# A hybrid recurrent and attention block on one core: two attention row blocks under way, and blocks of the second and third pair asked for at other times

## The chip, the cores and the metric

The kernel runs on one core of one Trainium2 chip. The metric is the device time of one execution in microseconds (us). Engines are named as in the profile: PE (TensorE matmul), PEld (its weight loads), DVE (VectorE), ACT (ScalarE), POOL (GpSimd) and SP (SyncE, which issues most DMAs).

## The reference

One layer of a streaming encoder. 16 learned tokens are put ahead of 512 input tokens, so T = 528, with 1024 features each. All is float32.

```python
u = rmsnorm(h, norm_mix)
proj = u @ w_in                                  # 1024 x 5384
feat_rw, feat_fx, gates = ...                    # 1792, 1544 and 2048 columns
y_rw = rwkv7_branch(feat_rw)                     # 8 heads of 64: a recurrence over all tokens
y_fx = fox_branch(feat_fx)                       # 8 heads of 64: causal attention with forgetting
g = sigmoid(gates + b_gate)
merged = g[:1024] * (y_rw @ w_out_rw) + g[1024:] * (y_fx @ w_out_fx)
h = h + merged @ w_o
h = h + square(relu(rmsnorm(h, norm_mlp) @ w_up)) @ w_down
```

The attention of one head: query and key are normalised over their 64 features; the logit of row q and column k gets F[q] - F[k], a running sum of log sigmoids, and a causal mask; then softmax and the product with the values. The recurrent branch updates a 64 x 64 state a token at a time: `S = S * w + (S a) b + v k`, `y = S r`.

## The kernel before

Products of the large matrices are float32 as three passes: each operand is split into a high half (written by ACT) and a low half (written by DVE), and high x high, high x low and low x high are added up on PE. Tokens lie along the free dimension.

The part that the change touches is the stage from about 30 to 423 us of the span. It holds nearly all of the projections by `w_in`, the attention and the recurrence. Heads are worked on in pairs, 128 features wide, four pairs (0 to 3 in the code; first to fourth in the text) in either branch. The recurrence takes its pairs two at a time, in two groups, since each group is one chain of nine chunks of 64 tokens.

The stage is written as streams: Python generators that emit instructions and yield what they need next, an event or a time. `Turns.run` (L165) is a planner: it keeps a model of the clock (`Clock`, L63), always lets the stream of the lowest rank go on whose need is met, and so fixes the order of PE's instructions, which PE then follows. The streams and their ranks:

- rank 0, `chain` (L917): the nine chunks of a group of the recurrence, in which PE, DVE and ACT take turns
- rank 1, `recurrent` (L1021): for each pair its decay, keys, rows and scores, then `inverse` (L843) of the group's small triangular matrices, which is work for DVE above all
- rank 2, `attention` (L608): for each pair, one after the other, the four row blocks of 128 queries. `scored(i)` (L622) multiplies queries and keys (L631) and does the softmax on DVE and ACT (L640 to L647); `turned(i, pes)` (L651) transposes the weights on PE (L661, L663) and copies them out (L666 to L669); `mixed` (L671) multiplies them by the values (L676, L679)
- rank 3, `fox_features` (L545): for each pair the normalised query and key (L573) and the transposed values (L599, L602)
- rank 4, `divided` (L534) and `group_norm` (L985), the latter with L1003 and L1006
- rank 8, `projections` (L480): 24 blocks of 128 columns of `w_in` for the branches and 16 blocks for the gates. This is the bulk of the matmuls (L506), and what the planner puts on PE where no other stream can go on

A block is asked for with `ask` (L450), which puts it into a list by rank: blocks of the recurrence 1, of attention 2, gates 9. `projections` takes the first of the list, and works ahead: while one block's matmuls go on, the next is being converted (L475 on ACT, L476 on DVE) and the one after it loaded (L462). A block may have a `need`, an event; when its turn comes and the event isn't done, `projections` waits there, with everything behind it.

What is asked when, before: each attention pair asks for its query, key and values when `fox_features` comes to it, so those of the second pair when the first pair's are done; those of the third and fourth pair after `fox_near[p - 2]`, which is set when the last row block of the pair two before has been scored. Buffers set this: query and key tiles have two, and the squares and values share a ring of two (tag `fsq`). The third pair's recurrent values are asked for when the first inverse is through, with the need that the first chain has read the old ones (`values_read[0]`).

In `attention` a row block is scored, then transposed, then the next one is scored.

After the stage come the output projections (L1097), `w_o` (L1128, L1158), the first half of the MLP (L1186) and the second (L1313). There the sums of `w_down` blocks (L1235) read tiles `traw`, 16 of which are loaded by POOL's own DMA queue (L1223).

The functions that the diff touches:

Of the kernel before, what the change touches and what calls it, by code (L numbers as in the profile page):

```python
# [19 lines left out]
T = 528  # L20
# [167 lines left out]
def kernel(ctx, tc, ht, x, win, par, cst, gain, lora, wout, wo, wup, wdn, out, dbg=None):  # L188
# [97 lines left out]
    with ExitStack() as st:  # L286
# [147 lines left out]
        def banks(n):  # L434
            return ck.ring("sm", n, 4)
# [98 lines left out]
        def divided():  # L534
# [7 lines left out]
            for k in range(2, 4):  # L542
                split(*two(0, k), y_rw[:, k, :])

        def fox_features():  # L545
            for p in range(4):
                b0 = B_PAIR + 6 * p
                if p > 1:
                    yield fox_near[p - 2]

                def ask_normed(blk, parts, name, need=None):
                    d = {}

                    def begin():
                        c0 = parts[0][0]
                        d["f"] = f = fp.tile([128, T - c0], F32, name=name, bufs=2)
                        d["sq"] = sq = fp.tile([128, T], F32, name="fsq", tag="fsq", bufs=2)

                        def evac(po, sl):
                            d["s"] = act(sq[:, sl], po, AF.Square)  # L560
                            A.copy(f[:, sl.start - c0:sl.stop - c0], po)
                        return evac
                    d["in"] = ask(2, blk, begin, parts, need)
                    return d

                def normed(d, parts, gcol):
                    yield d["in"]
                    f, sq = d["f"], d["sq"]
                    yield lambda: max(ck.ready(sq), banks(len(parts)))
                    pin = None  # L570
                    for a0, a1 in parts:
                        pq = psm("pssq")[:, :a1 - a0]
                        mm(pq, ones_blk, sq[:, a0:a1], start=True, stop=True)  # L573
                        pin = pin or pinned(d["s"])
                        after(act(sq[:, a0:a1], pq, AF.Ln, bias=eps, scale=1.0 / 64), pin)
                    c0 = parts[0][0]
                    act(sq[:, c0:], sq[:, c0:], AF.Exp, scale=-0.5)
                    V.scalar_tensor_tensor(f, f, gcol, sq[:, c0:], ALU.mult, ALU.mult)
                    return f

                whole = ((0, HT), (HT, T))
# [3 lines left out]
                def begin():  # L585
                    d["v"] = fp.tile([128, T], F32, name="vf", tag="fsq", bufs=2)
                    return lambda po, sl: A.copy(d["v"][:, sl], po)
# [5 lines left out]
                vf = d["v"]  # L593
                yield lambda: max(ck.ready(vf), banks(2))
                vt = fp.tile([128, 4, 128], F32, name="vt", bufs=2)
                vm = fp.tile([48, 128], F32, name="vm", bufs=2)
                pv = psm("pv")
                for j in range(4):
                    nc.tensor.transpose(pv[:, 128 * j:128 * j + 128], vf[:, NM + 128 * j:NM + 128 * j + 128], ident)  # L599
                A.copy(vt.rearrange("p a b -> p (a b)"), pv)  # L600
                pvm = psm("pvm")
                nc.tensor.transpose(pvm[:16, :128], vf[:, :NM], ident)  # L602
                for e, hs in enumerate(hss):
                    A.copy(vm[32 * e:32 * e + 16, hs], pvm[:16, hs])
                fox_tiles[p] = q, k, vt, vm
                fox_ready[p].done = True

        def attention():  # L608
            for p in range(4):
# [12 lines left out]
                def scored(i):  # L622

                    n = NM + 128 * (i + 1)
                    parts = [(0, n)] if n <= 512 else [(0, n - 256), (n - 256, n)]
                    yield lambda: max(ck.ready(q, k), banks(2 * len(parts)))
                    scs = [[], []]
                    for a, b in parts:
                        for e, hs in enumerate(hss):
                            sc = psm("psc")[:, :b - a]  # L630
                            mm(sc, q[hs, 128 * i:128 * i + 128], k[hs, a:b], start=True, stop=True)  # L631
                            scs[e].append((sc, a, b))
                    pes = []
                    for e in range(2):
                        pe = fp.tile([128, T], F32, name="pe", bufs=2)
                        nm = fp.tile([128, 2], F32, name="nm", bufs=3)
                        least = 3e38
                        for x, (sc, a, b) in enumerate(scs[e]):
                            if b == n:
                                V.tensor_tensor(sc[:, b - a - 128:], sc[:, b - a - 128:], cmask, ALU.add)  # L640

                            V.tensor_tensor_reduce(pe[:, a:b], sc, along[e][:, a:b], -1.0, least, ALU.add, ALU.min, nm[:, x:x + 1])
# [4 lines left out]
                        V.tensor_scalar(pe[:, :n], pe[:, :n], rsum, None, ALU.mult)  # L647
                        pes.append(pe)
                    return pes
# [77 lines left out]
        class Pair:  # L727
            def __init__(self, p):
                self.p, self.b0 = p, B_PAIR + 6 * p + 3
# [187 lines left out]
        def chain(g, prs):  # L917
# [21 lines left out]
            for c in range(NCH):  # L939
# [76 lines left out]

        inverted = [Event() for g in range(2)]
        values_read = [Event() for g in range(2)]
        chained = [Event() for g in range(2)]
# [425 lines left out]
```

## Time and profile before

| | us |
|---|---|
| median of 3 runs | 847.93 |
| lowest and highest run | 847.22, 848.41 |
| the profiled execution | 848.62 |
| its span, from the first to the last instruction | 846.8 |
| PE busy | 829.4 (98%) |
| DVE busy | 626.7 (74%) |
| ACT busy | 458.1 (54%) |
| POOL busy | 117.7 (14%) |
| mean granted clock | 0.996 |

The profile is of one execution. A row of a group of instructions reads: line, engine, operation, tile written and tiles read, shapes, count, then busy us, mean ns of one, idle us of the engine just before them, and what ended it. A row of the timeline reads: start us, us, engine, line, operation, tiles, count, and in brackets how long the engine had been idle and what it waited for. PE's matmuls overlap: the time that one takes to the next is shorter than its duration. A row of a stretch gives its length, the busy time of PE, PEld, DVE, ACT and POOL (with counts), the granted clock of PE, the share of the DMA engines and GB/s.

### The profile page before, as it was taken

Reading aid. Unit: us, or ns where it says so; the run is one execution under the profiler, and the core shown is the slowest. Engines: PE = TensorE matmul, PEld = TensorE weight load, DVE = VectorE, ACT = ScalarE, POOL = GpSimd, SP = SyncE. Lnnn points to the kernel's source line nnn. Section 1 sums busy time; section 2 is a strip of 40 time slices with the busy share of each in tenths; the row PEclk is TensorE's granted clock in tenths of the full one; section 3 lists DMA queues with packets and bytes.
Section 4 is the critical chain, followed back from the end, with each engine's and each line's share of the span. In section 5 each row is a group of like instructions: output and inputs, shape, how many; then the busy total and the mean of one; then the engine's idle time right before and its main releaser. Section 6 shows DMA issues by size and latency. Waiting matters only on the chain.

```text
span 846.8 us, 15315 instructions
## 1 busy us (share of the span) xinstructions
PE 829.4 (98%) x5752; PEld 681.9 (81%) x5752; DVE 626.7 (74%) x1227; ACT 458.1 (54%) x946; POOL 117.7 (14%) x121
## 2 busy tenths in 40 slices
PE   7899999999999999999899999999999999999998
PEld 6888977878878867877588889888888888888886
DVE  6996986679899457666467544875898679867988
ACT  7767537765764356655366432665345444543452
POOL 1010200001010000000022101200560065007300
PEclk9999999999999999999899999999999999999999
DMA  6131231202112231143577402640753175327531
GB/s 229 56 106 54 76 101 42 77 27 64 53 61 74 90 101 52 38 137 101 175 253 248 145 26 87 187 125 26 253 170 100 51 248 152 97 93 217 155 108 74
DMA packets 51482, 95.88 MB, mean 113 GB/s; under 512 B 5832, under 2 KB 7240, under 8 KB 51408
## 3 DMA queue, kind: packets, MB, share of 16 engines
q1 hardware_dynamic: 47680, 86.38, 32.1%
q0 software_dynamic: 1280, 4.20, 1.7%
q10 hardware_dynamic: 2448, 4.33, 1.5%
q8 instruction: 45, 0.74, 0.4%
q14 instruction: 29, 0.24, 0.1%
HBM read 88.57 MB, written 6.31 MB: 112 GB/s over the span
## 4 chain that ended last, share of the span: by engine, by line
PE 84%; DVE 7%; ACT 3%; issue 2%; DMA 1%; DVEq 0%; ACTq 0%
PE po L1186 21%; PE pj L506 21%; PE po L1313 12%; PE po L1097 5%; PE pd L1313 5%; PE po L1158 3%; PE pw L884 2%; PE py L679 1%; PE psc L631 1%; PE pd L1128 1%; PE po L1128 1%; PE ppt L663 1%; PE psr L831 1%; DVE wlo L476 1%; PE pch L950 1%
## 5 line engine op out<-in xcount | busy, mean ns | idle before, releaser
L506 PE MATMUL pj<-uhi,whi 128*128 128x264 f32 (+1 forms) x480 | 165.7, 345 | 0.0
L506 PE MATMUL pj<-ulo,whi 128*128 128x264 f32 (+1 forms) x480 | 154.0, 321 | 1.5 <-DVE ulo L406 1.5
L506 PE MATMUL pj<-uhi,wlo 128*128 128x264 f32 (+1 forms) x480 | 153.9, 321 | 0.0
L239 DVE TENSOR_TENSOR wlo<-wraw,whi 128x512 fp32r<-128x512 f32 x88 | 91.9, 1054 | 28.8 <-ACT whi L238 28.7
L506 PEld LDWEIGHTS pj<-uhi,whi 128*128 128x128 f32 x480 | 90.2, 188 | 14.4 <-issue 5.5
L506 PEld LDWEIGHTS pj<-ulo,whi 128*128 128x128 f32 x480 | 90.4, 188 | 8.4 <-DVE ulo L406 1.9
L506 PEld LDWEIGHTS pj<-uhi,wlo 128*128 128x128 f32 x480 | 90.3, 188 | 6.9
L1186 PE MATMUL po<-zhi,whi 128*128 128x512 f32 (+1 forms) x248 | 94.8, 382 | 0.0
L1186 PE MATMUL po<-zlo,whi 128*128 128x512 f32 (+1 forms) x248 | 94.8, 382 | 0.0
L1186 PE MATMUL po<-zhi,wlo 128*128 128x512 f32 (+1 forms) x248 | 94.8, 382 | 0.0
L238 ACT CAST whi<-wraw 128x512 fp32r<-128x512 f32 x88 | 53.8, 617 | 55.9 <-PE po L1186 23.5
L476 DVE TENSOR_TENSOR wlo<-wraw,whi 128x512 fp32r<-128x512 f32 x80 | 55.5, 699 | 27.1 <-ACT whi L475 26.7
L475 ACT CAST whi<-wraw 128x512 fp32r<-128x512 f32 x80 | 49.0, 617 | 42.3 <-PE pj L506 41.6
L273 ACT CAST whi<-t 128x512 fp32r<-128x512 f32 x64 | 39.9, 624 | 44.5 <-DVE wlo L274 27.2
L1313 PE MATMUL po<-wlo,fhi 128*128 128x512 f32 (+1 forms) x164 | 63.4, 387 | 0.1
L1313 PE MATMUL po<-whi,flo 128*128 128x512 f32 (+1 forms) x164 | 62.8, 384 | 0.0
L1313 PE MATMUL po<-whi,fhi 128*128 128x512 f32 (+1 forms) x164 | 62.3, 384 | 0.0
L274 DVE TENSOR_TENSOR wlo<-t,whi 128x512 fp32r<-128x512 f32 x64 | 43.6, 690 | 24.3 <-ACT whi L273 24.0
L1235 POOL TENSOR_TENSOR t<-traw 128x512 f32<-128x512 f32 x24 | 36.4, 1525 | 176.1 <-DMA traw<-in_wdn 175.5
L1186 PEld LDWEIGHTS po<-zhi,whi 128*128 128x128 f32 x248 | 46.6, 188 | 9.0
L1186 PEld LDWEIGHTS po<-zhi,wlo 128*128 128x128 f32 x248 | 46.6, 188 | 9.0
L1186 PEld LDWEIGHTS po<-zlo,whi 128*128 128x128 f32 x248 | 46.6, 188 | 9.0
(307 smaller groups left out, 1740.2 us busy)
## 6 DMA issues: line engine op xcount, KB each, us to landing
wraw<-in_win SPq DMA_DIRECT2D x84, 256.0 KB, 2.6
wraw<-in_wup SPq DMA_DIRECT2D x60, 256.0 KB, 3.0
wraw<-in_wdn SPq DMA_DIRECT2D x48, 256.0 KB, 2.6
traw<-in_wdn SPq DMA_DIRECT2D x48, 256.0 KB, 3.3
gd<-gt ACTq DMA_DIRECT2D x16, 256.0 KB, 2.3
wraw<-in_wout SPq DMA_DIRECT2D x16, 256.0 KB, 3.4
gl<-gd SPq DMA_DIRECT2D x16, 256.0 KB, 3.4
traw<-in_wdn POOLq DMA_DIRECT2D x16, 256.0 KB, 3.1
```

The source lines that it names most:

```text
L238: A.copy(hi, raw)
L239: low.tensor_tensor(lo, raw, hi.bitcast(F32), ALU.subtract)
L273: A.copy(hi, x)
L274: V.tensor_tensor(lo, x, hi.bitcast(F32), ALU.subtract)
L475: A.copy(hi, raw)
L476: low.tensor_tensor(lo, raw, hi.bitcast(F32), ALU.subtract)
L506: mm(po, a, b[:, k, a0:a1], start=n == 0, stop=n == 23)
L1097: mm(po, a, ys[k][:, b, :], start=n == 0, stop=n == 11)
L1158: mm(po, a[:, k, 128 * i:128 * i + 128], b[:, k, :], start=n == 0, stop=n == 23)
L1186: mm(po[:, t0:t1], a, b[:, k, t0:t1], start=n == 0, stop=n == 23)
L1235: eng.tensor_tensor(t, sums[c, pair] if c in (T1, T2) else c, d, ALU.add)
L1313: mm(x[i][:, cols], a[:, k, left, 128 * rows:128 * rows + 128], c[:, cols], start=start and k == 0 and n == 0, stop=stop and k == n_pairs ...
```

## The change

Five edits:

1. `fox_features` is split into a class. The first pair's three blocks are asked for at the start as before, and with them the second pair's query (it needs the first pair's key to be done, `k_done`) and key (it needs the first pair's values, `v_done`). The second pair's values are asked for when the loop comes to it. The third and fourth pair ask as before.
2. `attention` scores the next row block before it transposes the present one. `fox_near` is set ahead of the third block's transposes, not behind them.
3. The softmax tile gets two names, for even and odd row blocks, two buffers each, the even one 128 columns shorter.
4. The third pair's recurrent values are asked for by the chain itself, at the point where `values_read[0]` is set, without a need. `recurrent` waits for that event before it uses them.
5. The scratch for DMAs that POOL issues is 4096 instead of 8192.

```diff
         def fox_features():
-            for p in range(4):
-                b0 = B_PAIR + 6 * p
+            fox = [Fox(p) for p in range(4)]
+            fox[0].ask()
+            fox[0].ask_values()
+            fox[1].ask(fox[0].k_done, fox[0].v_done)
+            for p, x in enumerate(fox):
                 if p > 1:
                     yield fox_near[p - 2]
...
-                dq, dk, d = ask_normed(b0, SEQ, "qa", fox_done[p - 2] if p > 1 else None), ask_normed(b0 + 1, whole, "ka"), {}
-                q_done = Event()
...
-                v_in = ask(2, b0 + 2, begin, need=q_done)
-                q = yield from normed(dq, SEQ, qg8)
-                q_done.done = True
-                k = yield from normed(dk, whole, pr[:, C_KG:C_KG + 1])
-                yield v_in
+                    x.ask(fox_done[p - 2])
+                if p > 0:
+                    x.ask_values()
+                q = yield from x.normed(x.dq, SEQ, qg8)
+                x.q_done.done = True
+                k = yield from x.normed(x.dk, x.WHOLE, pr[:, C_KG:C_KG + 1])
+                x.k_done.done = True
+                yield x.v_in
...
+                x.v_done.done = True
                 fox_tiles[p] = q, k, vt, vm
                 fox_ready[p].done = True
...
-                        pe = fp.tile([128, T], F32, name="pe", bufs=2)
+                        pe = fp.tile([128, T if i % 2 else T - 128], F32, name=f"pe{i % 2}", bufs=2)
...
                 pes = yield from scored(0)
                 for i in range(4):
+                    if i < 3:
+                        nxt = yield from scored(i + 1)
+                        fox_near[p].done = i == 2
                     yield from turned(i, pes)
-                    if i < 3:
-                        pes = yield from scored(i + 1)
-                        fox_near[p].done = i == 2
+                    pes = nxt
                 yield from mixed()
...
                     if c == NCH - 2:
                         values_read[g].done = True
+                        if g == 0:
+                            seconds[0].ask_values()
...
+                    if j == 0 and g > 0:
+                        yield values_read[0]
                     yield q.v_in
...
                 if g == 0:
-                    pairs[2].ask_values(values_read[0])
+                    seconds.append(pairs[2])
                     yield from pairs[2].decay()
...
-    nc = bacc.Bacc("TRN2", target_bir_lowering=False, num_devices=1, dynamic_dma_scratch_size=8192)
+    nc = bacc.Bacc("TRN2", target_bir_lowering=False, num_devices=1, dynamic_dma_scratch_size=4096)
```

More of the change, by code (lines that the diff above doesn't have):

```diff
@@ L543, in divided, with __init__, ask_normed, begin @@
                 split(*two(0, k), y_rw[:, k, :])
-        def fox_features():
-            for p in range(4):
-                b0 = B_PAIR + 6 * p
+        class Fox:
+            WHOLE = ((0, HT), (HT, T))
+            def __init__(self, p):
+                self.b0 = B_PAIR + 6 * p
+                self.q_done, self.k_done, self.v_done = (Event() for i in range(3))
+            def ask_normed(self, i, parts, name, need):
+                d = {}
+                def begin():
+                    c0 = parts[0][0]
+                    d["f"] = f = fp.tile([128, T - c0], F32, name=name, bufs=2)
+                    d["sq"] = sq = fp.tile([128, T], F32, name="fsq", tag="fsq", bufs=2)
+                    def evac(po, sl):
+                        d["s"] = act(sq[:, sl], po, AF.Square)
+                        A.copy(f[:, sl.start - c0:sl.stop - c0], po)
+                    return evac
+                d["in"] = ask(2, self.b0 + i, begin, parts, need)
+                return d
+            def ask(self, need_q=None, need_k=None):
+                self.dq = self.ask_normed(0, SEQ, "qa", need_q)
+                self.dk = self.ask_normed(1, self.WHOLE, "ka", need_k)
+            def ask_values(self):
+                def begin():
+                    self.v = fp.tile([128, T], F32, name="vf", tag="fsq", bufs=2)
+                    return lambda po, sl: A.copy(self.v[:, sl], po)
+                self.v_in = ask(2, self.b0 + 2, begin, need=self.q_done)
+            def normed(self, d, parts, gcol):
+                yield d["in"]
+                f, sq = d["f"], d["sq"]
+                yield lambda: max(ck.ready(sq), banks(len(parts)))
+                pin = None
+                for a0, a1 in parts:
+                    pq = psm("pssq")[:, :a1 - a0]
+                    mm(pq, ones_blk, sq[:, a0:a1], start=True, stop=True)
+                    pin = pin or pinned(d["s"])
+                    after(act(sq[:, a0:a1], pq, AF.Ln, bias=eps, scale=1.0 / 64), pin)
+                c0 = parts[0][0]
+                act(sq[:, c0:], sq[:, c0:], AF.Exp, scale=-0.5)
+                V.scalar_tensor_tensor(f, f, gcol, sq[:, c0:], ALU.mult, ALU.mult)
+                return f
@@ L548, in fox_features @@
+        def fox_features():
+            fox = [Fox(p) for p in range(4)]
[3 more added lines that the diff above has]
+            for p, x in enumerate(fox):
                 if p > 1:
                     yield fox_near[p - 2]
[L551 to L579, printed above, removed]
@@ L581, in fox_features @@
-                whole = ((0, HT), (HT, T))
-                dq, dk, d = ask_normed(b0, SEQ, "qa", fox_done[p - 2] if p > 1 else None), ask_normed(b0 + 1, whole, "ka"), {}
-                q_done = Event()
-                def begin():
-                    d["v"] = fp.tile([128, T], F32, name="vf", tag="fsq", bufs=2)
-                    return lambda po, sl: A.copy(d["v"][:, sl], po)
-                v_in = ask(2, b0 + 2, begin, need=q_done)
-                q = yield from normed(dq, SEQ, qg8)
@@ L595, in fox_features @@
+                x.k_done.done = True
+                yield x.v_in
+                yield lambda: max(ck.ready(x.v), banks(2))
                 vt = fp.tile([128, 4, 128], F32, name="vt", bufs=2)
@@ L598, in fox_features @@
                 for j in range(4):
-                    nc.tensor.transpose(pv[:, 128 * j:128 * j + 128], vf[:, NM + 128 * j:NM + 128 * j + 128], ident)
+                    nc.tensor.transpose(pv[:, 128 * j:128 * j + 128], x.v[:, NM + 128 * j:NM + 128 * j + 128], ident)
                 A.copy(vt.rearrange("p a b -> p (a b)"), pv)
                 pvm = psm("pvm")
-                nc.tensor.transpose(pvm[:16, :128], vf[:, :NM], ident)
+                nc.tensor.transpose(pvm[:16, :128], x.v[:, :NM], ident)
                 for e, hs in enumerate(hss):
                     A.copy(vm[32 * e:32 * e + 16, hs], pvm[:16, hs])
+                x.v_done.done = True
                 fox_tiles[p] = q, k, vt, vm
@@ L1018 @@
         values_read = [Event() for g in range(2)]
+        seconds = []
         chained = [Event() for g in range(2)]
```

2 lines of the change are left out of this document (removed).

## The prediction

> **What bounds the kernel now.** I read the page first, then the chain of waits in order of time, then the busy time by stage, and last the instructions of the places that stood out. All times are microseconds from the start of the span.
>
> ```profile
> span 846.8 us, 15315 instructions
> PE 84%; DVE 7%; ACT 3%; issue 2%; DMA 1%; DVEq 0%; ACTq 0%
> ...
> 104.00:175.00 71.00, 69.88 (x841) 54.71 (x841) 49.33 (x136) 42.29 (x111) 0.14 (x1) 1.00 0.21 66
> 175.00:264.00 89.00, 88.34 (x843) 77.42 (x840) 80.77 (x201) 58.62 (x140) 8.77 (x13) 1.00 0.18 55
> 264.00:361.00 97.00, 96.53 (x1078) 74.11 (x1077) 60.98 (x174) 51.67 (x137) 0.00 (x0) 1.00 0.23 72
> 361.00:412.70 51.70, 51.70 (x260) 39.16 (x261) 31.64 (x97) 25.47 (x62) 0.00 (x0) 1.00 0.37 118
> 412.70:423.00 10.30, 8.04 (x32) 2.87 (x31) 3.59 (x11) 3.57 (x10) 0.00 (x0) 0.70 0.71 255
> ```
>
> The second row is the chain that ended last: 84% of it is PE. The five rows below are stretches: after the length come the busy times of PE, its weight loads, DVE, ACT and POOL, then the granted clock. PE is the bound. From 104 to 412.7 it idles 1.12 + 0.66 + 0.47 = 2.3 us in 308.7, so putting matmuls elsewhere there can win little. The one bad stretch is the last ten: 2.3 us idle in 10.3, and a clock of 0.70. Instruction by instruction, with the same steps of the third pair (365 to 381) above those of the fourth for comparison:
>
> ```profile
> 365.15 0.27 PE L661 MATMUL ppm<-cs,pe 128*16 128x128 f32 x1
> 365.61 0.49 PE L506 MATMUL pj<-uhi,whi 128*128 128x512 f32 x1
> ...
> 377.33 1.07 PE L676 MATMUL py<-pTm,vm 16*64 16x512 f32 x4
> 380.64 0.52 PE L631 MATMUL psc<-ka,qa 64*128 64x144 f32 x4
> ...
> 407.68 2.79 PE pj L506 x12
> 410.40 1.16 PE L631 MATMUL psc<-ka,qa 64*128 64x272 f32 x8
> 412.75 0.40 PE L506 MATMUL pj<-uhi,wlo 128*128 128x512 f32 x1
> 414.35 0.28 PE L661 MATMUL ppm<-cs,pe 128*16 128x128 f32 x1 [1.21 <-DVE pe L647]
> 414.47 0.60 PE L663 MATMUL ppt<-cs,pe 128*128 128x128 f32 x4
> 416.12 0.28 PE L661 MATMUL ppm<-cs,pe 128*16 128x128 f32 x1 [1.05 <-DVE pe L647]
> 416.77 1.86 PE L676 MATMUL py<-pTm,vm 16*64 16x512 f32 x4
> 418.56 4.54 PE L679 MATMUL py<-pT,vt 128*64 128x512 f32 x16
> 423.02 1.05 PE L1097 MATMUL po<-ys,whi 128*128 128x512 f32 x2
> ...
> 418.00:420.00 2.00, 2.00 (x6) 0.53 (x6) 0.00 (x0) 0.00 (x0) 0.00 (x0) 0.50 1.06 423
> ```
>
> The last pair's fourth row block is scored at 410.40, the last gate projection issues its last matmul at 412.75, and nothing is left to cover the softmax. PE waits twice for L647, and then the mixing matmuls, 3.31 us for the third pair (377.33 to 380.64), take 6.25 us (416.77 to 423.02), at half clock by the last row.
>
> **The change, part by part.** No matmul is added or taken away. What alters is the order in which the scheduler lays them down on PE, and PE runs them in that order.
>
> *Second pair's query and key asked for at the start, its values as soon as the first pair's features are issued.* These blocks are needed before the second pair can be scored; at the same time the projections are the cover of every other stream. Now three gates, which nothing needs before 423, run ahead of them (the first and the last of their evictions, L519):
>
> ```profile
> 113.26 0.68 ACT L519 ACTIVATE gt<-pj,pr 128x512 f32<-128x512 f32 x1
> ...
> 135.80 0.68 ACT L519 ACTIVATE gt<-pj,pr 128x512 f32<-128x512 f32 x1
> 149.10 0.58 ACT L561 COPY qa<-pj 128x512 f32<-128x512 f32 x1
> ...
> 171.10 1.00 PE py L676 x4
> ...
> 212.71 0.37 ACT L587 COPY vf<-pj 128x264 f32<-128x264 f32 x1
> ...
> 217.42 0.52 PE L631 MATMUL psc<-ka,qa 64*128 64x144 f32 x4
> ```
>
> The second pair's values come at 212.71 and its first scores at 217.42, though the first pair mixes at 171.1. After the change I expect query, key, one gate and the values in the four slots that end from 113 to 149, so that the second pair starts when the first is through, near 170: attention moves forward by some 217 - 170 = 47 us. Its end then lies near 423 - 47 = 376, and the gates that it has passed come behind it, with no other stream to wait for. That alone covers the tail, and a slip of up to 35 us of attention still would be covered. The new waits (second query behind the first key, second key behind the first values) stop the projections while they are unmet, with all gates queued behind and every stream's cover gone:
>
> ```profile
> 102.10 1.05 PE L573 MATMUL pssq<-fsq,cs 128*128 128x264 f32 x4
> ...
> 109.44 0.60 PE L599 MATMUL pv<-cs,vf 128*128 128x128 f32 x4
> ```
>
> The first key's normalising matmuls are issued at 102.1 and the first values' transposes at 109.4; the first slot begins about 113.3 - 5.6 = 107.7 (24 steps of 2.79 / 12) and the second at 113. Both waits are met: 0. Unmet, one would cost up to a block, 5.6 us.
>
> *Scores of the next row block ahead of the transposes of this one.* Even if attention stayed last, the fourth block's scores would stand ahead of the third's transposes, and the gate pieces that now run from 407.68 to 410.47 would cover its softmax. Both parts remove the same loss, so it counts once. The softmax tile, 128 columns shorter for even blocks, changes no instruction: 0.
>
> What the tail costs: the gate piece of 412.75 has had its step, 0.23, at 412.98. From there to 416.77 pass 3.79, in which the two groups of five transposes need 2 x 0.46 = 0.92 (365.15 to 365.61): 2.87 lost. The mixing loses 6.25 - 3.31 = 2.94. Together **-5.8**.
>
> [...]
>
> *DVE fuller in the middle.* From 175 to 264 DVE is busy 80.8 of 89.
>
> ```profile
> L642 DVE CUSTOM_DVE_ANT_0 pe<-psc,nF 128x272 f32<-128x272 f32 (+2 forms) x32 | 13.1, 437 | 3.7 <-PE psc L631 3.5
> L666 DVE COPY pT<-ppt 128x384 f32<-128x384 f32 (+2 forms) x32 | 13.9, 452 | 7.4 <-PE ppt L663 7.2
> ...
> 240.00:260.00 20.00, 19.74 (x182) 16.49 (x181) 18.97 (x41) 12.33 (x31) 1.25 (x2) 1.00 0.15 46
> 100.00:120.00 20.00, 19.41 (x158) 16.92 (x158) 19.05 (x46) 7.89 (x18) 0.00 (x0) 1.00 0.25 81
> ```
>
> The five attention lines (these two are the first and the last; L640, L646 and L647 lie between) hold 57 us of DVE in all, 14.3 a pair; three of the second pair's four blocks lie in this stretch already, 9.4 us. With all of that pair and a third of the next it would hold about 10 more, so DVE is full there and work slides right. Where DVE is 95% busy, PE idles 0.26 to 0.59 in 20 us; over 89 that is 1.2 to 2.6, of which 0.66 is there now. Bounds: -0.5 (the idle of the stretch from 264 to 361 goes as its DVE, 63% busy, gets lighter) to +2.0. I take **+1.2**, nearer the upper end, since the stretch will be as full as these two rows.
>
> *Switches between tile shapes.* Six steps of a projection take 0.73 behind a full-array transpose and 0.93 behind a 64-wide group:
>
> ```profile
> 149.58 0.73 PE pj L506 x6
> ...
> 153.04 0.93 PE pj L506 x6
> ```
>
> A switch is 0.2. Of the 32 score and transpose steps that move, if half lose or gain one, that is -3.2 to +3.2. The first and third pair took turns with the two recurrent chains before, the second and fourth would do so now: I take 0.
>
> *Third pair's recurrent values.* They were asked for ahead, behind a wait; now the chain asks for them when it has read the old ones, so they come behind the two blocks in hand, about 8 us later.
>
> ```profile
> 223.22 0.87 PE pyt L1003 x8
> ...
> 229.63 0.93 PE pbn L814 x2
> ```
>
> The bonus matmul (L814), the first to need them, also waits for the first group norm (L1003): hidden, 0; without that cover, up to 8.
>
> *DMA scratch halved.* It bears on the 16 DMAs of POOL's queue:
>
> ```profile
> 518.24 1.78 POOL L1223 DMA_DIRECT2D traw<-in_wdn  x3 [44.62 <-DVE zlo L1150]
> ...
> 559.01 16.34 PE po L1313 x72
> ...
> traw<-in_wdn POOLq DMA_DIRECT2D x16, 256.0 KB, 3.1
> ```
>
> Three go out at once, for three buffers, and nothing shows them waiting for the queue: 0. If each had to be issued (0.6) and to land (3.1, the median) before the next, 16 would take 59, to 577, where the third product, which reads the sums, begins at 559 + 2 x 5.4 = 570: up to +8 with the last sum.
>
> Sum: -5.8 + 1.2 = -4.6. Span 842.2; the profiled run takes 848.62, 1.82 outside its span, and lies 0.69 above the median of 847.93, so **843.3**.
>
> **The rivals.** (a) *The tail stays, shorter.* Attention is still last; PE waits little, but the array still slows. For it: attention ends last today. Against: the gates that now run first. The gaps go, the mixing stays slow: 847.9 - 2.87 + 1.2 = 846.3. [...]
> (b) *No change.* The scheduler still spends its gates early, under the denser attention, and the tail is as it is: 847.9.
> (c) *Slower: the row blocks stall in the middle.* The scheduler's clock books the low half of the weights (L476) on another engine than DVE, which does it; transposes are then laid down before their softmax is done, and PE, in order, waits as it does at 414.35. Nine such waits of 1.1 are 9.9: 847.9 - 5.8 + 9.9 = 852.0; it decides from seven (7.5 us lost). For it: DVE full from 175 to 264. Against: PE loses 0.66 there today. The scratch at +8 falls here too.
>
> **How the numbers follow.** What a measurement of this kernel can tell from no change is about 0.2%, 1.7 us. Main case 0.62; its own range, with the switches at either end, is 840.1 to 846.5. (a) 0.15, (b) 0.09, (c) 0.14. Faster means below 846.2: 0.60 of the main case and half of (a), 0.68. Slower, above 849.6, is nearly all of (c): 0.13. The rest is 0.19. The range takes in the main case, (a) and (b) with the highest run of before, 848.4, and leaves (c) out: 840.1 to 848.4.
>
> **What would show it.** Right: the last gates' evictions (L519) come after the last pair's mixing; the second pair's first scores near 170; no wait for L647 at the end of the stage; clock 1.00 up to L1097, which starts near 418. Wrong: PE waiting for attention's tiles between 170 and 260, mixing at half clock, or PE idle behind an unmet wait of the projections.

## The result, and the profile after

The changed kernel takes **842.58 us** (median of 6 runs, 839.94 to 844.54) against 847.77 for the kernel before beside it (6 runs, 847.22 to 848.41): a ratio of 0.9938, 95% interval 0.9918 to 0.9958. The prediction was 843.3. The profiled run of the changed kernel is the longest of its six, 844.54, with a span of 842.8.

The time agrees with the forecast, but the two sides of the sum do not. The stage with attention ends 8.1 us earlier, where 4.6 were forecast, and about a half of that is given back in this run right behind the stage, where no change was forecast. Lines of the changed kernel have other numbers than before: L519 stays, L560, L561 and L587 are now L562, L563 and L576, L631 is L648, L647 is L664, L676 and L679 are L693 and L696, L1091 to L1102 are L1114 to L1125, L1097 is L1120, L1128 and L1158 are L1151 and L1181.

The stretches of the stage, in the same columns as before (length, busy PE, PEld, DVE, ACT, POOL, granted clock):

```profile
104.00:175.00 71.00, 69.64 (x865) 54.88 (x864) 50.91 (x149) 44.64 (x120) 0.14 (x1) 1.00 0.20 60
175.00:264.00 89.00, 87.91 (x837) 74.79 (x836) 73.19 (x187) 57.16 (x137) 8.72 (x13) 1.00 0.20 61
264.00:361.00 97.00, 96.93 (x1074) 74.69 (x1073) 72.04 (x231) 57.14 (x160) 0.00 (x0) 1.00 0.22 70
361.00:407.00 46.00, 46.00 (x244) 35.85 (x243) 22.82 (x49) 20.04 (x39) 0.00 (x0) 1.00 0.35 110
407.60:417.90 10.30, 10.30 (x46) 8.39 (x45) 2.40 (x4) 3.28 (x6) 0.00 (x0) 1.00 0.47 139
```

The last row lies across the stage's end at 414.95, and it holds no idle time and no slow clock. The second pair's first scores in the timeline, then the chain of waits at the end of the stage, then the first issue of the output projections:

```profile
168.93 0.52 PE L648 MATMUL psc<-ka,qa 64*128 64x144 f32 x4
...
363.88 1.00 PE py L693 x4
366.50 1.45 PE py L696 x12
367.95 14.10 PE pj L506 x60
383.63 6.95 PE pj L506 x30
392.17 22.95 PE pj L506 x99
...
414.95 0.62 PE L1120 MATMUL po<-ys,whi 128*128 128x512 f32 x2
```

The last pair mixes at 363.88 to 367.95, and dense gate projections are the end of the stage.

Behind the stage stands what the prediction did not look at. A gate is stored to memory when it is evicted (gd from gt, on ACT's queue) and read back for the output projections (gl from gd, L1114). Eight merged blocks are made from 16 of these reads with two buffers per branch; the last of them, `mhi` (L1125), is needed by the first half of `w_o` (L1151). First before, then after, the first read-back in SP's timeline and the last `mhi` in ACT's; for the kernel after, two waits of PE in its timeline as well:

```profile
423.16 1.75 SPq L1091 DMA_DIRECT2D gl<-gd  x4
473.65 0.63 ACT L1102 ACTIVATE mhi<-gl 128x512 fp32r<-128x512 f32 x1 [3.27 <-POOL gl L1101]
```

```profile
419.73 1.75 SPq L1114 DMA_DIRECT2D gl<-gd  x4
460.56 0.50 PE L1151 MATMUL po<-whi,mhi 128*128 128x512 f32 x1 [1.11 <-DVE gl L1122]
470.60 0.63 ACT L1125 ACTIVATE mhi<-gl 128x512 fp32r<-128x512 f32 x1 [2.55 <-POOL gl L1124]
473.21 0.49 PE L1151 MATMUL po<-whi,mhi 128*128 128x512 f32 x1 [1.55 <-ACT whi L238]
```

From the first read to the last block pass 50.5 before (473.65 - 423.16) and 50.9 after, while PE's output projections need 43.6 to 44.0. The reads begin 0.1 behind the stage's end before and 4.8 behind it after (419.73 - 414.95). So the last block comes 6.6 after PE is through with them before, where the first half of `w_o` takes it without a wait, and 12.0 after it now, where PE waits twice. The second wait is for a block of `w_o`, not for `mhi`: ACT writes that block's high half (L238) only at 472.54, behind the last `mhi` and a table load of 1.28. The busy time of PE in 20 us around that place, before and after:

```profile
468.00:488.00 20.00, 20.00 (x90) 16.57 (x89) 10.25 (x17) 9.08 (x16) 1.73 (x2) 1.00 0.40 124
```

```profile
460.00:480.00 20.00, 17.65 (x73) 13.42 (x74) 11.95 (x18) 11.34 (x19) 4.11 (x2) 1.00 0.59 189
```

### The profile page after: what moved, and what is told of

Its sections match the earlier page's. It is cut to its first block, busy times and chain, and to the rows that moved or that the text cites. A ratio compares the mean times of both kernels' runs of the same rounds, so it can differ in the third digit from the quotient of the medians.

```text
span 842.8 us, 15298 instructions
## 1 busy us (share of the span) xinstructions
PE 824.7 (98%) x5752; PEld 679.5 (81%) x5752; DVE 612.6 (73%) x1227; ACT 458.1 (54%) x946; POOL 121.8 (14%) x121
## 4 chain that ended last, share of the span: by engine, by line
PE 81%; DVE 5%; ACT 4%; DMA 3%; issue 2%; POOL 1%; SPq 0%; DVEq 0%; ACTq 0%; POOLq 0%
PE pj L506 23%; PE po L1209 21%; PE po L1336 12%; PE pd L1336 5%; PE po L1181 3%; PE pw L902 2%; PE psc L648 1%; PE py L696 1%; PE psr L849 1%; POOL gl L1124 1%; PE ppt L680 1%; PE pch L968 1%; PE pssq L586 1%; PE pvt L948 1%; DMA gl<-gd 1%
## 5 line engine op out<-in xcount | busy, mean ns | idle before, releaser
L239 DVE TENSOR_TENSOR wlo<-wraw,whi 128x512 fp32r<-128x512 f32 x88 | 81.8, 941 | 42.4 <-ACT whi L238 42.4
L238 ACT CAST whi<-wraw 128x512 fp32r<-128x512 f32 x88 | 53.7, 617 | 59.2 <-PE po L1209 25.2
L476 DVE TENSOR_TENSOR wlo<-wraw,whi 128x512 fp32r<-128x512 f32 x80 | 55.6, 699 | 22.7 <-ACT whi L475 22.3
L274 DVE TENSOR_TENSOR wlo<-t,whi 128x512 fp32r<-128x512 f32 x64 | 43.6, 690 | 24.3 <-ACT whi L273 24.0
L1225 ACT CAST fhi<-R 128x768 fp32r<-128x768 f32 (+1 forms) x32 | 30.2, 945 | 45.3 <-DVE R L1232 23.0
```

The source lines that it names most:

```text
L238: A.copy(hi, raw)
L239: low.tensor_tensor(lo, raw, hi.bitcast(F32), ALU.subtract)
L274: V.tensor_tensor(lo, x, hi.bitcast(F32), ALU.subtract)
L476: low.tensor_tensor(lo, raw, hi.bitcast(F32), ALU.subtract)
L1225: A.copy(fhi[:, j, a:b], R[:, a:b])
```

## The experiments

The profiled executions by stage, us. "Ends" is the start of the output projections, "behind" the span less that; the idle time of PE is that of the three stretches from 104 to 361, as in the rows above. "From 60" is the time from one and the same instruction, the scores matmul of the recurrence that starts at 60.04 in the kernel before (L831), to "ends": all kernels run the same PE instructions up to 118. "Shapes" counts how often two neighbouring matmuls of the stage differ in tile shape (as 128\*128 and 64\*64). "Lag" is how long after PE's last output projection the last `mhi` is written, and "waits" is PE's idle time in the 110 us behind the stage.

| kernel | ends | from 60 | PE idle 104 to 361 | shapes | lag | waits | behind | span |
|---|---|---|---|---|---|---|---|---|
| before | 423.0 | 363.0 | 2.25 | 306 | 6.6 | 0.1 | 423.8 | 846.8 |
| after | 415.0 | 354.9 | 2.52 | 293 | 12.0 | 3.0 | 427.8 | 842.8 |
| after, again | 414.3 | 354.8 | 2.50 | 293 | 9.9 | 2.1 | 426.5 | 840.8 |
| early blocks alone | 415.1 | 356.1 | 2.28 | 302 | 9.7 | 2.0 | 426.1 | 841.2 |
| reorder alone | 419.2 | 359.8 | 5.39 | 309 | 9.1 | 2.2 | 426.7 | 845.9 |
| reorder alone, second look | 419.1 | 359.7 | 5.31 | 309 | 9.2 | 2.4 | 429.0 | 848.1 |
| reorder in the last pair | 417.1 | 357.5 | 2.25 | 306 | 9.7 | 1.2 | 425.4 | 842.5 |
| the same, third buffer | 416.5 | 357.5 | 2.22 | 306 | 9.8 | 1.3 | 425.5 | 842.0 |
| after without edit 4 | 415.3 | 356.2 | 2.98 | 297 | 9.6 | 1.4 | 425.7 | 841.0 |
| after, early read-backs | 414.9 | 354.9 | 2.54 | 293 | 9.0 | 1.0 | 424.7 | 839.6 |
| after, third buffer | 414.5 | 354.9 | 2.47 | 293 | 7.9 | 0.1 | 423.6 | 838.1 |
| after, both | 414.5 | 354.8 | 2.49 | 293 | 9.9 | 1.2 | 425.6 | 840.1 |
| before, early read-backs | 422.8 | 363.2 | 2.25 | 306 | 5.3 | 0.1 | 423.7 | 846.5 |
| before, third buffer | 418.7 | 360.0 | 2.18 | 306 | 8.4 | 0.6 | 424.8 | 843.4 |

"From 60" repeats better than "ends". The five profiles with the changed kernel's stage agree in it to 0.1, and before with early read-backs differs from before by 0.2, while "ends" of one stage differs by 0.7 and more for what happens ahead of 60. So gains of the stage are best read in the second column: 8.1 for the whole change.

### First: the parts apart, and the read-back

Four kernels beside 29 runs of the kernel before (median 847.4).

*The reorder alone*: the kernel before with edits 2, 3 and 5.

```diff
                 for i in range(4):
+                    if i < 3:
+                        nxt = yield from scored(i + 1)
+                        fox_near[p].done = i == 2
                     yield from turned(i, pes)
```

> The kernel of before with only the row blocks reordered (scores of the next one ahead of the transposes; the two softmax tiles and the smaller DMA scratch, which make room for them). Blocks are asked for as before. If the reorder alone covers the tail: no wait for L647 at the end of the stage, mixing at full clock, stage end 5 to 6 us earlier than 423, time 847.8 - 5.8 = about 842. The stage ends with attention, not with a gate, so nothing should be given back behind it. Rival, that the early blocks are what covers the tail: time within 1.5 us of before.

Measured: 849.11 (12 runs, 847.52 to 850.78), ratio 1.0026 (1.0013 to 1.004). The tail is covered, as the step said: the stage ends 3.8 earlier, 3.2 of them behind 60. But the kernel is slower. Its stretches, then its waits of PE (us in total, times, longest):

```profile
104.00:175.00 71.00, 69.07 (x840) 54.23 (x839) 47.80 (x133) 42.24 (x107) 0.14 (x1) 1.00 0.20 66
175.00:264.00 89.00, 85.54 (x809) 75.35 (x809) 73.18 (x191) 56.15 (x136) 7.05 (x11) 1.00 0.19 64
```

```profile
PE pch L945 <- DVE uv L968: 1.8, 2, 1.4
PE pup L761 <- DVE Bm L833: 1.0, 1, 1.0
PE pch L951 <- DVE Rs L947: 0.8, 2, 0.6
```

PE idles 1.93 + 3.46 = 5.4 there instead of 1.8, waiting for the recurrence's tiles. DVE was not full (73 of 89). That its work came in another order, with the chain's later, is the likely reading; no run shows it apart. A further 2.9 go behind the stage. That is much like rival (c), with waits for the recurrence in place of attention's.

*The early blocks alone*: the changed kernel with the row blocks in the old order and one softmax tile (edits 2 and 3 undone).

```diff
                 for i in range(4):
+                    yield from turned(i, pes)
                     if i < 3:
-                        nxt = yield from scored(i + 1)
+                        pes = yield from scored(i + 1)
                         fox_near[p].done = i == 2
-                    yield from turned(i, pes)
-                    pes = nxt
```

> The changed kernel with the row blocks in the old order (transposes, then the next scores, one softmax tile). If the early blocks alone cover the tail, as the prediction had it (attention some 47 us earlier, gates last): no half clock, stage end at about 417 or earlier, time 841 to 845. If they need the reorder with them: attention is still last, and the time stays above 845.

Measured: 843.26 (12 runs), ratio 0.9963 (0.995 to 0.9977). Most of the gain is here. From 60 on the stage is 6.9 shorter than before, with both parts 8.1: though the two end at nearly the same time (415.05 and 414.95), this profile was 1.1 ahead at 60 already. The reorder, which loses 0.26% by itself, seems to add some 0.3% when the second pair's blocks are early: the whole change measured 0.9938 (0.9918 to 0.9958), which overlaps with this, and 0.9928 (0.9916 to 0.994), below, which doesn't. The stage says the same, with 1.2 more.

*The first four read-backs asked for ahead*, into a buffer of their own.

```diff
+        glx = yp.tile([128, 4, S], F32, name="glx", tag="y_fx")
+        for n in range(4):
+            nc.sync.dma_start(glx[:, n, :], gates_d[8 * (n % 2) + n // 2])
...
+                if m < 2:
+                    g = glx[:, 2 * m + br, :]
+                else:
```

> The changed kernel, and the gates' first four read-backs (for the first two column blocks of the output projection) go into a buffer of their own that is free before the stage ends, so they do not wait for the last gate. Theory: the changed kernel gains 8 us by the end of the stage (414.9 against 423.0) and gives 4 back behind it, because these loads wait for the last gate's store; then PE waits behind 455 go and the time is 838 to 840, with a spread under 2 us. Rival, that the giving back is the DMA engines' bandwidth with the weights of the output projection late: a gain of 1 to 2 us at most (1 MB moved out of a stretch of some 275 GB/s would be 3.8 us if it were all bandwidth, and the same would then show in before).

Measured: 841.02 (6 runs, 839.96 to 842.58), ratio 0.9932 (0.9913 to 0.9951). The theory that the late start of the reads is the loss gave too much: the gain on the changed kernel is within the intervals. With the first four reads issued from 369.84 on, one wait of 1.0 for gl stays in the first half of `w_o`. So the start of the reads is not all; the loop's pace has to be looked at.

*The same in the kernel before.*

> The kernel of before with the same four read-backs ahead. There PE shows no wait behind the stage, so by the theory of the wait: the same time as before, within 1 us. If the stretch were short of bandwidth in itself, it could gain only where PE waits, and none of that shows: also no change; a gain above 1.5 us would say that matmul busy time hides stalls there.

Measured: 847.74 (12 runs), ratio 1.0008 (0.9995 to 1.0021). Before the change, the read-back holds nothing up.

### Second: the pace of the read-back

The kernel before beside these: 17 runs, median 848.14.

*The changed kernel again*, as a base for these.

> The changed kernel once more, beside the two below. All theories: 841 to 844, as measured; in the profile the first half of w_o again takes more than the 21.8 us of before.

Measured: 841.94 (5 runs, 840.98 to 842.54), ratio 0.9928 (0.9916 to 0.994). In its profile the stage ends 8.7 earlier than before, and 2.7 are given back, in two waits of 1.2 and 0.9 and in the matmuls around them. So the 4.0 of the first profile is the large end.

*A third buffer for each branch's gates.*

```diff
-                g = mp.tile([128, S], F32, name=f"gl{br}", bufs=2)
+                g = mp.tile([128, S], F32, name=f"gl{br}", bufs=3)
```

> The changed kernel with three buffers instead of two for the gates' read-backs, which still wait for the last gate's store. Theory now (the first version, that only the start of the loads counts, gave 3.2 of 4.3 us in the profile but little in the median): the read-backs are a loop of load, tanh, two sums and release whose two buffers let eight column blocks take 50 us, whatever PE does; PE needs 44. In the kernel before the loop starts with the stage and its lag of 7 us is hidden in the first half of w_o; in the changed one it starts 4.7 us later, and PE waits. Three buffers shorten the loop: first half of w_o back to about 22 us, time 838.5 to 840.5. Rival, bandwidth of the DMA engines in this stretch: no gain beyond 1 us, since the same bytes move.

Measured: 840.84 (5 runs, 839.78 to 841.72), ratio 0.9915 (0.9903 to 0.9927). SP's and ACT's timelines, and the busy times around the start of `w_o`:

```profile
419.71 2.70 SPq L1114 DMA_DIRECT2D gl<-gd  x6
465.96 0.63 ACT L1125 ACTIVATE mhi<-gl 128x512 fp32r<-128x512 f32 x1 [0.35 <-POOL gl L1124]
457.00:477.00 20.00, 20.00 (x89) 16.20 (x88) 14.40 (x22) 11.40 (x20) 2.90 (x2) 1.00 0.55 182
```

The reads start as late as ever, but the loop takes 46.3 instead of 50.9; PE has no wait left, and what lies behind the stage is as long as before (423.6 against 423.8). In this profile the faster loop took the waits away. In the medians it is worth 1.1 us over the changed kernel, and the intervals (0.9903 to 0.9927, 0.9916 to 0.994) overlap a little.

*Both*: early read-backs and the third buffer.

> Both remedies: the first four read-backs ahead in a buffer of their own, three buffers for the rest. By the theory of the loop: as with three buffers or up to 1 us better, 838 to 840, since nothing is left to wait for. By bandwidth: between the changed kernel and the one with the four loads ahead, 840.5 to 842.

Measured: 840.26 (5 runs, 839.46 to 841.84), ratio 0.9912 (0.9901 to 0.9924): no different from the third buffer alone. These two have the lowest medians found. But its profile waits again, 0.9 for gl and 0.2 for a weight, though the reads start early and three buffers stand ready. Over all profiles the lag goes with the waits: PE idles 0.1 to 0.6 behind the stage where the lag is 5.3 to 8.4, and 1.0 to 3.0 where it is 9.0 to 12.0. What sets the lag is open: neither the start of the reads nor the number of buffers does by itself.

*The third buffer in the kernel before*, with edit 5 for the room.

> The kernel of before with three read-back buffers and, to make room for them, the smaller DMA scratch of the change. PE shows no wait behind the stage there, so by the theory of the loop no gain: within 1 us of before. It also shows the scratch alone: if POOL's 16 loads had to go one by one the first slice of the MLP would take up to 8 us longer; expected 0.

Measured: 848.04 (12 runs), ratio 1.0005 (0.9991 to 1.002). Neither the buffer nor the halved scratch changes the kernel before. By accident its profile splits the tail's two losses. PE's timeline:

```profile
412.94 0.28 PE L661 MATMUL ppm<-cs,pe 128*16 128x128 f32 x1 [1.21 <-DVE pe L647]
414.71 0.28 PE L661 MATMUL ppm<-cs,pe 128*16 128x128 f32 x1 [1.05 <-DVE pe L647]
415.35 1.07 PE L676 MATMUL py<-pTm,vm 16*64 16x512 f32 x4
416.36 2.37 PE L679 MATMUL py<-pT,vt 128*64 128x512 f32 x16
418.66 0.74 PE L1097 MATMUL po<-ys,whi 128*128 128x512 f32 x2
```

The same two waits, but the mixing takes 418.66 - 415.35 = 3.31, as the third pair's does, and not 6.25: here the clock stayed up (1.00 from 412 to 422). That puts the half clock at 2.94, as the step had it. (The stage ends 4.4 earlier than in the profile of before; the other 1.4 arise ahead of 60.)

### Third: what else can be taken apart

The kernel before beside these: 28 runs, median 847.37.

*The changed kernel without edit 4*: the third pair's recurrent values are asked for ahead again.

```diff
-                        if g == 0:
-                            seconds[0].ask_values()
...
-                    if j == 0 and g > 0:
-                        yield values_read[0]
...
-                    seconds.append(pairs[2])
+                    pairs[2].ask_values(values_read[0])
```

> The changed kernel with the third pair's recurrent values asked for as before (early, with a wait). In the changed kernel they came 30 us later than before and the second chain started 9 us later. If that is hidden behind the gates, as the prediction had it: the changed kernel's time, 841 to 843. If the late values cost something by fewer turns between streams: 1 us better or more.

Measured: 843.94 (11 runs, 842.39 to 845.82), ratio 0.996 (0.9948 to 0.9973), against 0.9928 (0.9916 to 0.994) and 0.9938 (0.9918 to 0.9958) with it. So edit 4 is worth 0.2 to 0.3%, the second interval overlapping with this one. PE's waits from 104 to 264, first without it, then with it:

```profile
PE pbt L856 <- DVE KT L814: 1.3, 1, 1.3
PE pup L778 <- ACT sg L258: 0.8, 1, 0.8
```

```profile
PE pg L1026 <- ACT fsq L588: 1.0, 1, 1.0
PE pup L778 <- ACT sg L258: 0.8, 1, 0.8
```

Its profile shows the loss in the stage: from 60 on it takes 356.2 instead of 354.8 to 354.9, 1.3 to 1.4 more, of which 0.5 are idle time; what lies behind it is no longer.

*The reorder in the last pair only*: the kernel before with edits 3 and 5, and the next block scored first in the fourth pair alone.

```diff
+                    if i < 3 and p == 3:
+                        nxt = yield from scored(i + 1)
                     yield from turned(i, pes)
+                    if i < 3 and p < 3:
+                        nxt = yield from scored(i + 1)
...
```

> The kernel of before with the row blocks reordered in the fourth pair alone, where the tail is. The reorder in all pairs lost 3.6 us more than before by PE waiting for DVE between 104 and 264, beside the first chain, and gave no gain. Theory: those waits come from the first pair's row blocks, so here they are as before (about 2 us), the tail is covered, and the stage ends 5 to 6 us earlier, of which the read-back loop (its start can only move from 423.2 to about 420) leaves 2 to 4: 844 to 846. Rival, that the reorder itself is of no use in the tail: 847 to 848.

Measured: 844.36 (12 runs, 843.27 to 846.84), ratio 0.9974 (0.9961 to 0.9988). The middle is as it was before, and the tail is covered:

```profile
104.00:175.00 71.00, 69.90 (x849) 54.70 (x847) 49.28 (x137) 42.15 (x111) 0.14 (x1) 1.00 0.20 66
175.00:264.00 89.00, 88.34 (x840) 77.44 (x837) 80.74 (x202) 58.29 (x139) 8.75 (x13) 1.00 0.17 55
...
361.00:417.10 56.10, 56.10 (x289) 40.93 (x288) 35.27 (x104) 28.43 (x70) 0.00 (x0) 1.00 0.37 119
```

The stage ends 5.9 earlier (417.13 against 423.02), of which 0.4 arose ahead of 60: measured alone, the tail is worth 5.5, near the 5.8 that the prediction took off for it. 1.6 are given back behind the stage, and the median gains 3.

*The reorder alone, a second look* (one run of the first kernel above).

> A second look at the kernel of before with all row blocks reordered, to see where a run near its median of 849.1 (its profile was of 847.7) loses its time: in the waits for DVE between 104 and 264 (more than the 5.4 us idle of the first profile), or behind the stage, in the two stages from L1098 to L1129, which took 68.7 us in the first profile against 65.8 of the kernel before.

Measured: 849.89, span 848.1. The same idle time in the middle (1.86 + 3.45 = 5.3), the stage's end at 419.1, and 429.0 behind it. The loss in the middle repeats to 0.1 us; what goes behind the stage does not, 426.7 and 429.0. A part of that is the clock, whose mean is 0.997 in this profile and 1.0 in the first. The first three `pd` steps of the first half of `w_o` (L1129) start 0.4 apart (468.4, 468.8, 469.2), the last three 0.2 (489.4, 489.6, 489.8). This half lasts 25.2 (464.9 to 490.1) against 23.2 in the first profile; the waits in it make up 0.6 of the difference (1.6 against 1.0), which leaves some 1.4 for the clock, an estimate.

*The reorder in the last pair, with the third buffer.*

> The last kernel but one with three read-back buffers. By the theory of the loop it gives up to 3 us over two buffers, 842 to 844; this is what the covered tail alone is worth, about 5 us, without any block being asked for earlier. If the time stays with that of two buffers, the loop is not what holds it.

Measured: 844.79 (11 runs), ratio 0.9973 (0.9963 to 0.9984): the third buffer gives nothing here. In PE's waits one of 1.0 for gl stays. The lag is 9.8 here, and 9.7 with two buffers. So what the loop costs depends on more than its buffers, and why a wait stays here where the profile with the third buffer had none stays open.

## Why the prediction was right or wrong

**The tail, -5.8: right, and shown.** The loss is gone, and the reorder in the last pair takes 5.5 off the stage by nothing but covering it. The two halves, 2.87 of gaps and 2.94 of clock, are borne out by the one profile in which the gaps came without the slow clock. Why the clock fell is not shown. In the profile of before PE was idle for 2.3 of the 3.8 us ahead of the mixing, in two waits of 1.21 and 1.05, and the clock was 0.54 from 416.77 to 418.50 and 0.50 from there to the stage's end. In the kernel before with the third buffer the same two waits come, and the clock is 1.00 from 412 to 422. In the second look at the reorder, steps at about half rate come in the first half of `w_o`, which has waits of 0.5 and 1.1. So these waits do not settle by themselves whether the clock falls. The runs fit that: 12 of 74 of the kernel before show no half clock in their mean, as the last section tells.

**How it comes about: right.** The second pair's first scores come at 168.93 (170 was forecast), its blocks take the first four slots with one gate between, and the projections stop nowhere: there is no unmet need. ACT's timeline, with the first query, the gate, the first and second half of the values, and the last gate:

```profile
113.80 0.58 ACT L563 COPY qa<-pj 128x512 f32<-128x512 f32 x1
...
141.44 0.69 ACT L519 ACTIVATE gt<-pj,pr 128x512 f32<-128x512 f32 x1
149.42 0.38 ACT L576 COPY vf<-pj 128x264 f32<-128x264 f32 x1
155.80 0.36 ACT L576 COPY vf<-pj 128x264 f32<-128x264 f32 x1
...
415.45 0.68 ACT L519 ACTIVATE gt<-pj,pr 128x512 f32<-128x512 f32 x1
```

Attention ends at 368, 8 before the forecast 376, and the gates follow.

**"Both parts remove the same loss, so it counts once": right for the tail, wrong as the whole account of the reorder.** The reorder in all pairs has an effect in the middle: 3.1 us of waits without the early blocks, and with them a stage shorter by 1.2 and perhaps a gain of some 0.3%. Rival (c), which had 0.14, is what the reorder does by itself. That the early blocks take it away is measured; how they do it was not tried. Rivals (a) and (b) fall with the tail: it is neither shorter nor as it was, but gone.

**DVE full in the middle, +1.2: the step failed.** DVE is busy 73.2 of 89 there, not full; before it was 80.8. The prediction brought attention forward and left the recurrence where it was, but the recurrence's second group slid. In ACT's timeline, the third attention pair's query, the second half of its key, and the second half of the third pair's recurrent values:

```profile
207.89 0.59 ACT L562 ACTIVATE fsq<-pj 128x512 f32<-128x512 f32 x1
...
223.63 0.41 ACT L562 ACTIVATE fsq<-pj 128x264 f32<-128x264 f32 x1
...
233.29 0.49 ACT L322 ACTIVATE tm<-pj,pr 128x264 f32<-128x264 f32 x1
```

Before, these values were evicted at 197.32 and 202.98, so they come 30 us later, where 8 were forecast. The chain asks for them in its eighth chunk, at nearly the same time as that chunk came before (190.07 against 188.19), but then they stand behind the block under way and behind the query and key above, which took some 8 and 16 us in this stretch, not a block's 5.6. DVE's work moved to the next stretch (72.0 against 61.0 of 97), where there was room. But the late values are only a part of it: in the changed kernel without edit 4 DVE has written them by 208.3, and DVE is still busy no more than 75.4 of 89. So they account for 2.2 of the 7.6 that left the stretch; the rest was not traced. PE's idle time from 104 to 361 rose from 2.25 to 2.52: +0.3, not +1.2.

**Third pair's recurrent values, "about 8 us later, hidden, 0": mis-sized and the wrong sign.** They come 30 us later, as above, and no wait for them shows; but the edit isn't neutral, since with it the stage is 1.3 to 1.4 shorter and the kernel 0.2 to 0.3% faster.

**Switches between tile shapes, 0: mis-sized, within its bounds.** Of the 8.1 that the stage gains, 5.8 are the tail and -0.3 the idle time; 2.6 are left, inside PE's busy time. The changes of shape fall from 306 to 293, and at the step's 0.2 each 13 are 2.6. For the other kernels the same sum compares as follows:

| kernel | changes of shape against before | at 0.2 each | left over in the stage |
|---|---|---|---|
| after | 13 fewer | 2.6 | 2.6 |
| after without edit 4 | 9 fewer | 1.8 | 1.7 |
| early blocks alone | 4 fewer | 0.8 | 1.1 |
| reorder in the last pair | same | 0 | -0.4 |
| reorder alone | 3 more | -0.6 | 0.5 |

So the change doesn't trade one turn for another, as the step had it: it leaves fewer of them, and the gain goes with their number, to about 0.4 but for the reorder alone, which is 1.1 off. That they are the cause is likely and not shown, since no run changed the switches alone. The 0.2 itself is loosely founded: what stands ahead of the row at 149.58 is not a full-array transpose but L930, a 128\*64 group.

**Scratch and softmax tile, 0: right.** The kernel before with the halved scratch doesn't differ (1.0005, 0.9991 to 1.002). The +8 end did not come. The softmax tile has no run of its own; the reorder in the last pair has it too, and its stretches up to 361 are those of before.

**What was not in the sum.** It ended at the stage's end and took all that follows as moved by the same amount. What follows was not free to move: the gates' round trip through memory is a loop of 49 to 51 us in the changed kernel's two profiles, beside 44 of PE, and before it ended just in time for `w_o`. With gates as the last work of the stage, the reads also wait for the last gate's store (SP 2.5 us, by its waits), so the loop starts 4.8 after PE instead of 0.1. That the last block comes late and PE waits for it is shown; how much of it is the late start and how much the loop's pace is not. The give-back of 2.7 to 4.0 in the profiles was as large as the stage's unforeseen gain of 3.5, and so the total came out near. The sum was right by luck, by two errors of opposite sign.

## What to carry to other kernels

When a stage is made to end earlier, look at the first consumer behind it: a loop that ran just fast enough, fed by what is now produced last, can take a part of the gain back, as 2.7 to 4.0 us in the changed kernel's two profiles. More buffers are a cheap cure to try, though here they brought no gain clear of the noise. Of a reorder, ask in each place where it acts: here one order won 5.5 us in the last pair, where nothing else was to be done, and lost 3 in the middle, where another chain needed its turn. A total that comes out as forecast does not show that the terms did; compare stage by stage, and from an instruction that all the profiles share, since what happens ahead of it differs from run to run, by 0.7 us in the changed kernel's two profiles.

## What was not expected of the hardware

By the mean granted clock, the half clock at the end of the stage does not come in every run of the kernel before: 6.25 us at 0.50 take 0.0037 off the mean of a span of 846.8, and the profile of before has 0.996. Of the 74 runs of it beside the experiments, 12 have a mean granted clock of 0.999 or 1.0 and take 843.4 to 845.8 us, with their middle at 844.4; 56 have 0.996 or less, with their middle at 847.9, 3.5 above; 6 lie between. All 11 runs of the changed kernel have 0.999 or 1.0. So some 3 of the 5 us that the change gains are the tail's clock (an estimate, from the 3.5 between these runs and the 2.94 of the mixing), and they are had in most runs but not in all: beside the 12 runs without the half clock, the change gains only 2 to 2.5 (841.9 and 842.6 in its two sets).

The changed kernel itself spreads from 839.9 to 844.5 at a clock of 0.999 to 1.0. Its two profiles differ by 0.7 up to the stage's end, all of it ahead of 60, and by 1.3 behind it; what makes the loop of the read-backs faster or slower from run to run stays open.
